# Cached pages with half of their keys already turned, and the samples' partial sums kept in DRAM

## The chip, the cores and the metric

The kernel runs on one core of one Trainium2 chip. The metric is the device time of one execution in microseconds. Three runs of the kernel before took 866.78, 866.91 and 869.01 us, median 866.91.

The engines named below: TensorE (PE in the profile; PEld is its weight load), VectorE (DVE), ScalarE (ACT), GpSimd (POOL) and SyncE (SP). SP computes nothing here: it issues most of the DMAs. GpSimd issues the others, and computes as well.

## The reference

One inference step of a decoder of two layers, for a prompt (512 tokens) and for eight samples of four tokens each, with the same weights. The change touches only the samples' part of the second layer: attention over a paged cache of 4,096 latent rows for each sample (32 pages of 128 rows, chosen by a page table) and over the four new rows. A row has 256 latent elements (`ckv`), which serve as keys and as values, and 64 rotary elements (`krope`), which serve as keys alone.

```python
ckv_past = cache_ckv[page_table].reshape(db, past, KV_RANK)        # 8 x 4096 x 256
krope_past = cache_krope[page_table].reshape(db, past, QK_ROPE)    # 8 x 4096 x 64
...
def mla_attend(q_lat, q_rope, ckv, krope, qpos, kpos):
    s = (jnp.einsum('bthc,bsc->bhts', q_lat, ckv)
         + jnp.einsum('bthr,bsr->bhts', q_rope, krope)) * MLA_SCALE
    mask = kpos[None, :] <= qpos[:, None]
    s = jnp.where(mask[None, None], s, -1e30)
    p = jax.nn.softmax(s, axis=-1)
    return jnp.einsum('bhts,bsc->bthc', p, ckv)
```

For one sample there are 32 queries (8 heads x 4 tokens). All is float32.

## The kernel before

**The whole.** Activations are kept transposed, features on the 128 partitions. Most products of the prompt are done as three float32r matmuls of a high and a low part (`mm3`, L92). Layer A and the start of layer B run first, in an order that the framework's scheduler sets by simulated times. From L915 on, the orders of TensorE and of SP are fixed by the program as it is written out (`pe_order`, `sp_order`); VectorE, ScalarE and GpSimd are still scheduled.

**The woven stage.** From L915 several threads (Python generators) are written out in turns by `weave` (L930): a thread yields the TensorE time that its step is reckoned to take and the time after which its next step may come; the thread that is furthest behind its share is taken next. The threads are `round_scores` and `round_values` (the samples' paged attention), `gates_late` (four gate projections), then `head_inputs` and `heads` (the prompt's eight heads), then `out_all` (the output projection). So the steps of the rounds stand between those of the other threads on TensorE, in a fixed order.

**A round.** There are 16 rounds: eight samples, two rounds each, 16 pages a round. A round is loaded in two halves of eight pages (`load_half`, L971). A half has one tile `nat`, 128 partitions x 8 pages x 320 columns (256 latent, 64 rotary); `nats` has four buffers, two rounds' worth. SP reads the eight page numbers from the list in SBUF into registers (L974), with a check of each against its bounds, and issues one DMA a page (L978). A page row is 1,280 bytes. The halves of round n + 2 are issued where `round_values` of round n has read the same buffers for the last time.

- `turn_keys` (L994): the latent rows have to be turned for the score matmul, whose contraction is over the latent elements. Four 128x128 transposes on TensorE (`transpose`, L133) into a PSUM bank `tr`, then a copy to an SBUF tile `kt` by ScalarE or VectorE (`kt_evac`, L983; two to one). A half needs four such groups: two parts of the latent dimension (k) by two groups of four pages (jp). `kt` has six buffers.
- scores (L1021, L1030): 16 matmuls a half into one bank `ac`: eight with the turned keys `kt` and the queries `QT`, 256 columns each, and eight with the rotary columns of `nat` (which are stored turned) and `Qr`.
- softmax of the round (L1039 to L1041): row maximum on VectorE, exponential with its sum on ScalarE into `rt`.
- values (L1051 to L1064): four transposes of the weights, a copy, and 16 matmuls with `nat` itself. The trace counts these f32 score and value matmuls twice each.
- after a sample's first round, ScalarE copies the sum to `ostore[:, b, :]`; after its second, VectorE rescales it and adds the second (L1083, L1084). `ostore` is one SBUF tile, 128 x 8 x 256.

**The end.** `combine` (L1436) merges the four page groups, the two rounds and the four new rows of all samples with `ostore` (L1495); `sample_out` (L1544) and `out_rows` (L1342) project. Weight slabs come by SP (`slab`, L1308); each is split into a high part by ScalarE and a low part by GpSimd (L88, L89). `mix_b` (L1294) splits the gated rows of the heads. Pools are stacks in SBUF: a pool that is opened after another has closed takes its memory, and waits for what used it.

**The host's side.** `_layouts` (L1610) rearranges the inputs before the launch; `cache_P` is the cache of pages with `ckv` and the turned `krope` side by side.

Of the kernel before, what the change touches and what calls it, by code (L numbers as in the profile page):

```python
# [7 lines left out]
F32 = mybir.dt.float32  # L8
# [20 lines left out]
PGW = 320  # L29
ULEN = PAD + SEQ + NB * (PAD + NT)  # L30
# [7 lines left out]
def trunk_kernel(ctx: ExitStack, tc: tile.TileContext, A, O):  # L38
# [751 lines left out]
    pg = Pool("pg", "right", g=(N, 9))  # L790
# [9 lines left out]
    nc.sync.dma_start(pages, A["page_list"])  # L800

# [166 lines left out]
    loaded, scored = {}, {}  # L968
    n_pool = A["cache_P"].shape[0]

    def load_half(n, ih):  # L971
        t = nats("nat").rearrange("p (s x) -> p s x", s=8)
        c = (2 * n + ih) * 8
        loads, own = nc.values_load_multi_w_load_instructions(  # L974
            pages[:, c : c + 8], [mybir.EngineType.SP], min_val=0, max_val=n_pool - 1
        )
        for g in range(8):
            nc.sync.dma_start(t[:, g, :], A["cache_P"][bass.ds(own[g], 1)].rearrange("n p x -> p (n x)"))  # L978
        loaded[n, ih] = t, now[0] + 9.0
# [10 lines left out]
    def round_scores():  # L990
        for n, (b, r) in enumerate(rounds):
            nat, kt = [None, None], {}

            def turn_keys(ih, k, jp):  # L994
                ps = ps_("tr")
                for g in range(4):
                    transpose(ps[:, g * P : (g + 1) * P], nat[ih][:, 4 * jp + g, k * P : (k + 1) * P])
                x = pro("kt")
                kt_evac(x, ps)
                kt[ih, jp, k] = x  # L1000
                return 0.44, 0.8

            ss = None
            for ih in range(2):
                if nat[ih] is None:
                    yield lambda: (n, ih) in loaded and loaded[n, ih][1] <= now[0]
                    nat[ih] = loaded[n, ih][0]
                for k in range(2):
                    for jp in range(2):
                        if (ih, jp, k) not in kt:  # L1010
                            yield turn_keys(ih, k, jp)
                if ih == 0 and (n, 1) in loaded and loaded[n, 1][1] <= now[0]:
                    nat[1] = loaded[n, 1][0]
                    yield turn_keys(1, 0, 0)
                else:
                    yield 0.0, 0.8
                ss = ss or ps_("ac")
                o = ss[:, ih * 256 : (ih + 1) * 256]
                for k in range(2):
                    for j in range(4):  # L1020
                        nc.tensor.matmul(  # L1021
                            o[j * NS : (j + 1) * NS, :],
                            lhsT=QT[:, k, b, :],
                            rhs=kt[ih, j // 2, k][:, j % 2 * 256 : (j % 2 + 1) * 256],
                            start=k == 0,
                            stop=False,
                        )
                for f in range(2):
                    for j in range(4):
                        nc.tensor.matmul(  # L1030
                            o[j * NS : (j + 1) * NS, :].rearrange("p (i f r) -> p f i r", i=2, f=2)[:, f],
                            lhsT=Qr[:, b, f, :],
                            rhs=nat[ih][:, 2 * j : 2 * j + 2, 256:],
                            start=False,
                            stop=f == 1,
                        )
                yield 1.3, 0.0
# [6 lines left out]
    def round_values():  # L1044
        first_part = None
        for n, (b, r) in enumerate(rounds):
# [9 lines left out]
            for i in range(4):  # L1056
                for j in range(4):
# [3 lines left out]
                        rhs=nat[i // 2][:, 2 * j + i % 2, :256],  # L1061
# [7 lines left out]
            if r == 0:  # L1069
                nc.scalar.copy(ostore[:, b, :], po[:, :256])  # L1070
                first_part = nx, sm
            else:
# [10 lines left out]
                nc.vector.tensor_scalar_mul(ostore[:, b, :], ostore[:, b, :], w[:, 2:3])  # L1083
                nc.vector.scalar_tensor_tensor(  # L1084
                    out=ostore[:, b, :], in0=po[:, :256], scalar=w[:, 3:4], in1=ostore[:, b, :], op0=ALU.mult, op1=ALU.add
                )
            yield 0.86, 0.0
# [29 lines left out]
    rs = Thread(round_scores(), 0.0, 1.0, 98.0)  # L1117
# [314 lines left out]
    cb = Pool("cb", "right", c=(96, 3), ws=(D, 5))  # L1432
# [3 lines left out]
    def combine(cb, v):  # L1436
# [7 lines left out]
        ms = pro("kt")  # L1444
# [19 lines left out]
        selw = pro("kt")  # L1464
# [6 lines left out]
        tz = pro("kt")  # L1471
# [11 lines left out]
        tt = pro("kt")  # L1483
# [3 lines left out]
        for bq in range(2):  # L1487
            for r in range(2):
                for b4 in range(4):
                    b = bq * 4 + b4  # L1490
                    if r == 0:
                        lhsT, rhs = selw[:, b * NS : (b + 1) * NS], ostore[:, b, :]
# [9 lines left out]
        on = pro("kt")  # L1502
# [5 lines left out]
        oT = pro("kt")  # L1508
# [22 lines left out]
        ov = pro("kt")  # L1531
# [78 lines left out]
def _layouts(a):  # L1610
# [29 lines left out]
                    a["cache_krope"].reshape(-1, 2, 64, 64).transpose(0, 1, 3, 2).reshape(-1, P, 64),  # L1640
                ],
# [75 lines left out]
```

## Time and profile before

| | |
|---|---|
| median of three runs | 866.91 us (866.78 to 869.01) |
| the profiled execution's own time | 867.66 us |
| its span, first to last instruction | 865.8 us |
| mean granted TensorE clock | 0.990 |
| bytes moved | 139.46 MB, of which pages 256 x 160 KB |
| the stage with the page rounds, from the first page load | 485.0 to 796.7 us |

How to read it: the page's first part gives the time each engine was busy. A row of its fifth part is a group of equal instructions: line, engine, operation, out<-in by the program's names, sizes and count; behind the bar the busy time, the mean in ns of one, and the idle time of the engine just before them with what ended it. Matmuls are pipelined, so what one costs in a row of others is the distance of their starts in the timeline and not its duration. The stage table gives each engine's busy time between two times; the waits list who waited for whom. In a timeline row the first number is the start and the second the time to the end of the merged piece, both in us. SPq and POOL rows with DMA are issues; the transfer follows on 16 DMA engines.

### The profile page before, as it was taken

To read this page: it belongs to the slowest core of one execution; us is meant where nothing else is said; L and a number is where in the kernel's file an instruction comes from. 1 tells how busy PE (TensorE), PEld (TensorE's weight loads), DVE (VectorE), ACT (ScalarE), POOL (GpSimd) and SP (SyncE) were. 2 spreads that over 40 slices of the span, in tenths; PEclk is the share of its full clock that TensorE was granted. 3 is DMA by queue.
4 is the path that set the end of the run, shared out by engine and by line. 5 is a ranking of instruction groups with operands and counts; after the bars stand their busy time and mean duration, and the time that the engine had idled before them with its cause. 6 is when DMAs were issued, how large, how long until landed. Compare 5 with 4: busy or idle time off the path is not lost.

```text
span 865.8 us, 18559 instructions
## 1 busy us (share of the span) xinstructions
PE 823.7 (95%) x7162; PEld 711.3 (82%) x7162; DVE 514.9 (59%) x961; ACT 349.9 (40%) x693; POOL 257.9 (30%) x206
## 2 busy tenths in 40 slices
PE   6999999989999999989999999989999999999996
PEld 6989989988999989769998986767778777777764
DVE  7766665987843444966766445575665657631603
ACT  7453433322433243444343235454544545442212
POOL 0044222633343323305323227150331400034421
PEclk9999999999999999999999999999999999999999
DMA  8355167311332326447228665645646564674742
GB/s 308 93 191 208 49 210 247 113 56 40 110 92 92 102 100 207 141 147 265 90 85 306 196 200 184 194 149 164 190 142 183 147 178 129 208 244 139 269 171 103
DMA packets 80858, 139.46 MB, mean 161 GB/s; under 512 B 9057, under 2 KB 49762, under 8 KB 80514
## 3 DMA queue, kind: packets, MB, share of 16 engines
q1 hardware_dynamic: 76258, 123.53, 44.8%
q0 software_dynamic: 4512, 14.75, 4.9%
q8 instruction: 56, 0.92, 0.4%
q14 instruction: 32, 0.26, 0.1%
HBM read 129.53 MB, written 8.72 MB: 160 GB/s over the span
## 4 chain that ended last, share of the span: by engine, by line
PE 51%; issue 7%; DVE 6%; DMA 3%; ACT 3%; SPq 1%; POOL 1%; POOLq 0%; ACTq 0%; DVEq 0%
PE pa L93 8%; PE pa L95 8%; PE pa L94 8%; PE tr L134 6%; PE oa L93 2%; PE ac L1021 2%; PE oa L94 2%; PE oa L95 2%; PE ac L1058 2%; PE ac L1030 1%; DVE t L744 1%; DMA wr<-in_w_mem_v 1%; SPq L978 1%; DMA ws<-in_w_out_b 1%; DMA wr<-in_w_out_b 1%
## 5 line engine op out<-in xcount | busy, mean ns | idle before, releaser
L93 PE MATMUL pa<-h,wh 128*128 128x272 f32 x832 | 241.6, 293 | 4.8 <-DVE g L612 4.5
L95 PE MATMUL pa<-h,wl 128*128 128x272 f32 x832 | 238.5, 291 | 1.9 <-POOL wl L89 1.9
L89 POOL TENSOR_TENSOR wl<-wr,wh 128x1024 fp32r<-128x1024 f32 (+1 forms) x67 | 156.5, 2337 | 249.6 <-ACT wh L88 233.0
L94 PE MATMUL pa<-h,wh 128*128 128x272 f32 x640 | 185.6, 291 | 0.0
L93 PEld LDWEIGHTS pa<-h,wh 128*128 128x128 f32 x832 | 158.2, 191 | 9.3 <-issue 5.2
L95 PEld LDWEIGHTS pa<-h,wl 128*128 128x128 f32 x832 | 157.0, 190 | 4.3 <-POOL wl L89 2.6
L88 ACT CAST wh<-wr 128x1024 fp32r<-128x1024 f32 (+1 forms) x87 | 87.7, 1009 | 166.0 <-PE pa L94 56.0
L94 PEld LDWEIGHTS pa<-h,wh 128*128 128x128 f32 x640 | 122.3, 191 | 1.0
L134 PE MATMUL tr<-c,nat 128*128 128x128 f32 x512 | 79.2, 280 | 5.3 <-DVE kt L988 3.9
L134 PEld LDWEIGHTS tr<-c,nat 128*128 128x128 f32 x512 | 59.1, 141 | 20.5 <-issue 7.3
L986 ACT COPY kt<-tr 128x512 f32<-128x512 f32 x86 | 50.4, 590 | 58.5 <-PE tr L134 58.0
L260 DVE SCALAR_TENSOR_TENSOR g<-t,g 128x272 f32<-128x272 f32 x48 | 50.0, 1048 | 14.4 <-ACT t L259 14.2
L94 PE MATMUL pa<-g,wh 128*128 128x272 f32 x192 | 54.5, 288 | 0.1
L259 ACT ACTIVATE t<-g 128x272 f32<-128x272 f32 x48 | 20.3, 429 | 73.0 <-DVE g L246 71.7
L988 DVE COPY kt<-tr 128x512 f32<-128x512 f32 x42 | 28.8, 686 | 23.2 <-PE tr L134 22.9
L93 PE MATMUL oa<-wh,c 128*128 128x512 f32 x96 | 39.8, 414 | 0.0
L94 PE MATMUL oa<-wl,c 128*128 128x512 f32 x96 | 38.0, 395 | 1.1 <-POOL wl L89 1.1
L246 DVE SCALAR_TENSOR_TENSOR g<-pa,r 128x272 f32<-128x272 f32 x42 | 18.1, 437 | 31.3 <-PE pa L95 31.3
L94 PEld LDWEIGHTS pa<-g,wh 128*128 128x128 f32 x192 | 36.1, 188 | 0.3 <-DVE g L89 0.3
L1021 PE MATMUL ac<-kt,c 128*32 128x256 f32 x512 | 35.6, 392 | 0.1
L89 DVE TENSOR_TENSOR wl<-wr,wh 128x1024 fp32r<-128x1024 f32 x20 | 24.5, 1224 | 12.8 <-ACT wh L88 12.7
L89 DVE TENSOR_TENSOR q<-q,q 128x512 fp32r<-128x512 f32 x16 | 25.2, 1574 | 11.2 <-ACT q L88 11.1
(367 smaller groups left out, 1706.1 us busy)
## 6 DMA issues: line engine op xcount, KB each, us to landing
nat<-in_cache_P SPq DMA_DIRECT2D x256, 160.0 KB, 3.0
wr<-in_w_in_a SPq DMA_DIRECT2D x24, 512.0 KB, 3.8
wr<-in_w_in_b SPq DMA_DIRECT2D x19, 512.0 KB, 3.7
cs<-in_mem_kT SPq DMA_DIRECT2D x16, 512.0 KB, 5.3
wr<-in_w_out_a SPq DMA_DIRECT2D x16, 384.0 KB, 3.0
wr<-in_w_out_b SPq DMA_DIRECT2D x12, 512.0 KB, 4.0
ws<-in_w_out_b SPq DMA_DIRECT2D x12, 512.0 KB, 5.6
wr<-in_w_mem_k SPq DMA_DIRECT2D x8, 512.0 KB, 3.9
```

Of the source, the lines that this page charges most:

```text
L88: nc.scalar.copy(h, src)
L89: (eng or nc.vector).tensor_tensor(out=l, in0=src, in1=fr(h), op=ALU.subtract)
L93: nc.tensor.matmul(out, lhsT=wh, rhs=xh, start=start, stop=False)
L94: nc.tensor.matmul(out, lhsT=wh, rhs=xl, start=False, stop=False)
L95: nc.tensor.matmul(out, lhsT=wl, rhs=xh, start=False, stop=stop)
L134: nc.tensor.transpose(out, in_, ident[:k, :k])
L246: nc.vector.scalar_tensor_tensor(out=out[:, o : o + HALF], in0=ps[:, :HALF], scalar=scale, in1=bc[:, o : o + HALF], op0=ALU.mult, op1=ALU. ...
L259: nc.scalar.activation(th[:, :HALF], z[:, o : o + HALF], AF.Tanh)
L260: nc.vector.scalar_tensor_tensor(out=z[:, o : o + HALF], in0=th[:, :HALF], scalar=1.0, in1=z[:, o : o + HALF], op0=ALU.add, op1=ALU.mult,)
L986: nc.scalar.copy(out, src)
L988: nc.vector.tensor_copy(out, src)
L1021: nc.tensor.matmul(o[j * NS : (j + 1) * NS, :], lhsT=QT[:, k, b, :], rhs=kt[ih, j // 2, k][:, j % 2 * 256 : (j % 2 + 1) * 256], start=k == ...
```

## The change

**Pages.** The host now lays the latent rows of a page a second time into `cache_P`, turned: a row of the cache has 576 columns, 320 as before and 256 of turned keys. Of the eight pages of a half, the first four are loaded with all 576 columns (2,304 bytes a row) into a tile `a`, the last four with 320 into a tile `b`. Scores of the first four read the turned keys from `a`, without transposes and copies; the last four are turned as before. So a half needs two groups of transposes where it had four. `kt` has three buffers.

**Partial sums.** `ostore` is a DRAM tensor. A sample's sum is kept in a small tile `os` (two buffers); after the second round GpSimd writes it to DRAM, for the first seven samples. At the end SP reads the seven back with one DMA into a tile `o`; the eighth is used where it is.

**Page list.** The list is clamped once on VectorE when it comes in, and the checks of each page number on SP are gone.

**Small moves.** `pg` has eight buffers instead of nine; the tiles of `mix_b` come from other pools; the tiles of `combine` come from a pool `cb` that is opened after the page tiles are closed; the planner's reckoning of a load and the rounds' share of its time are other numbers.

The diff, cut to its core:

```diff
@@ sample page list
 nc.sync.dma_start(pages, A["page_list"])
+n_pool = A["cache_P"].shape[0]
+nc.vector.tensor_scalar(out=pages, in0=pages, scalar1=0, scalar2=n_pool - 1, op0=ALU.max, op1=ALU.min)
@@ pools of the rounds
-pro = Pool("pro", "right", kt=(512, 6), rt=(512, 3), os=(2048, 1))
-nats = Pool("nats", "right", nat=(8 * PGW, 4))
+pro = Pool("pro", "right", kt=(512, 3), rt=(512, 3), os=(256, 2))
+nats = Pool("nats", "right", a=(4 * PGK, 4), b=(4 * PGW, 4))
-ostore = pro("os").rearrange("p (b c) -> p b c", b=NB)
+ostore = dram.tile([NB - 1, P, 256], F32, name="ostore")
@@ load_half
-t = nats("nat").rearrange("p (s x) -> p s x", s=8)
+half = [nats(tag).rearrange("p (s x) -> p s x", s=4) for tag in "ab"]
...
+    skip_runtime_bounds_check_because="the list is clamped on the chip when it comes in",
...
 for g in range(8):
-    nc.sync.dma_start(t[:, g, :], A["cache_P"][bass.ds(own[g], 1)].rearrange("n p x -> p (n x)"))
-loaded[n, ih] = t, now[0] + 9.0
+    t = half[g // 4][:, g % 4, :]
+    nc.sync.dma_start(t, A["cache_P"][bass.ds(own[g], 1), :, : t.shape[-1]].rearrange("n p x -> p (n x)"))
+issued[0] = max(issued[0], now[0]) + 6.4
+loaded[n, ih] = half, issued[0] + 5.0
@@ round_scores
 for k in range(2):
-    for jp in range(2):
-        if (ih, jp, k) not in kt:
-            yield turn_keys(ih, k, jp)
+    if (ih, k) not in kt:
+        yield turn_keys(ih, k)
...
-rhs=kt[ih, j // 2, k][:, j % 2 * 256 : (j % 2 + 1) * 256],
+rhs=(nat[ih][0][:, :, PGW + k * P : PGW + (k + 1) * P] if j < 2 else kt[ih, k])[
+    :, j % 2 * 2 : j % 2 * 2 + 2, :
+],
@@ round_values, after a sample's second round
+if b < NB - 1:
+    nc.gpsimd.dma_start(ostore[b], part)
+else:
+    parts[b] = part
@@ the planner
-rs = Thread(round_scores(), 0.0, 1.0, 98.0)
+rs = Thread(round_scores(), 0.0, 1.0, 70.0)
@@ mix_b
-    mixed[k] = split(pc("c", F32R), pt("t", F32R, SEQ), t)
+    mixed[k] = split(pc("c", F32R), pat("p", F32R), t)
-    mixed[k] = split(pc("c", F32R), pg("g", F32R, SEQ), gt[k][:, :SEQ])
+    mixed[k] = split(pc("c", F32R), (pg("g", F32R) if k else pt("t", F32R))[:, :SEQ], gt[k][:, :SEQ])
@@ sample_out
+o = cb("o").rearrange("p (b c) -> p b c", b=NB - 1)
+nc.sync.dma_start(o, ostore.rearrange("b p c -> p b c"))
+parts.update({b: o[:, b, :] for b in range(NB - 1)})
@@ _layouts, third part of cache_P
+a["cache_ckv"].reshape(-1, P, 2, P).transpose(0, 3, 2, 1).reshape(-1, P, 256),
```

What stands where, at three places. On TensorE, before, the first half's scores of the third round (turned keys `kt`, rotary columns of `nat_6386`), then the values of the second round, then the next transposes of a page tile:

```order
L1021 MATMUL ac_6760<-kt_6663,c_4069 32x256 x2
L1021 MATMUL ac_6760<-kt_6685,c_4069 32x256 x2
L1021 MATMUL ac_6760<-kt_6692,c_4069 32x256 x2
L1021 MATMUL ac_6760<-kt_6699,c_4069 32x256 x2
L1030 MATMUL ac_6760<-nat_6386,c_4070 32x2x64 x8
L1058 MATMUL ac_6777<-nat_5785,rt_6721 32x256 x8
L1058 MATMUL ac_6777<-nat_5867,rt_6721 32x256 x8
L134 MATMUL tr_6967<-c_79,nat_6476 128x128 x4
```

The same scores after the change (`a_6132` and `b_6133` are the half's two tiles):

```order
L1028 MATMUL ac_6444<-a_6132,c_4069 32x256 x2
L1028 MATMUL ac_6444<-kt_6301,c_4069 32x256 x2
L1028 MATMUL ac_6444<-a_6132,c_4069 32x256 x2
L1028 MATMUL ac_6444<-kt_6389,c_4069 32x256 x2
L1039 MATMUL ac_6444<-a_6132,c_4070 32x2x64 x2
L1039 MATMUL ac_6444<-b_6133,c_4070 32x2x64 x2
L1039 MATMUL ac_6444<-a_6132,c_4070 32x2x64 x2
L1039 MATMUL ac_6444<-b_6133,c_4070 32x2x64 x2
L135 MATMUL tr_6461<-c_79,b_6168 128x128 x4
```

Four of the eight score matmuls read the page tile itself, and there are two `kt` tiles where there were four; the second round's values stand earlier, ahead of these scores.

On SP, before, from the last page of the first half to the first of the second (`c_4072` is the page list; ISA rows are register and check instructions):

```order
L978 DMA nat_5621<-in_cache_P 128x320
L974 TENSOR_LOAD c_4072
L974 ISA x16
L978 ISA
L978 DMA nat_5703<-in_cache_P 128x320
```

And after:

```order
L985 DMA b_5623<-in_cache_P 128x320
L976 TENSOR_LOAD c_4072
L985 ISA
L985 DMA a_5649<-in_cache_P 128x576
L985 ISA
```

The 16 check instructions ahead of a half's first DMA are gone, 512 in all; the DMAs keep their places and their count.

On GpSimd, before, ahead of the first output slab's low part (`wl`), with the turned queries of the last heads (`qr`) and two loads of gates kept in DRAM:

```order
L1210 TENSOR_TENSOR qr_9901<-t_9893,qr_9901 64x512
L1210 TENSOR_TENSOR qr_9904<-t_9893,qr_9904 64x512
L1297 DMA tab_11983<-gmd 128x512
L1297 DMA tab_11989<-gmd 128x512
L89 TENSOR_TENSOR wl_11670<-wr_11667,wh_11669 128x1024
L89 TENSOR_TENSOR wl_11684<-wr_11681,wh_11683 128x1024
```

And after:

```order
L1224 TENSOR_TENSOR qr_8584<-t_8576,qr_8584 64x512
L1224 TENSOR_TENSOR qr_8587<-t_8576,qr_8587 64x512
L1098 DMA ostore<-os_8706 128x256
L1098 DMA ostore<-os_9196 128x256
L90 TENSOR_TENSOR wl_9519<-wr_9516,wh_9518 128x1024
L90 TENSOR_TENSOR wl_9533<-wr_9530,wh_9532 128x1024
```

The stores of the sixth and seventh sample's sums now stand there, and the two loads of gates behind the first slabs.

More of the change, by code (lines that the diff above doesn't have):

```diff
@@ L960, in ps_ @@
         return (rb if tag in rb.tags else hb)(tag)
-    pro = Pool("pro", "right", kt=(512, 6), rt=(512, 3), os=(2048, 1))
-    nats = Pool("nats", "right", nat=(8 * PGW, 4))
+    pro = Pool("pro", "right", kt=(512, 3), rt=(512, 3), os=(256, 2))
+    nats = Pool("nats", "right", a=(4 * PGK, 4), b=(4 * PGW, 4))
     stats_m = cst([P, NB])
     stats_s = cst([P, NB])
-    ostore = pro("os").rearrange("p (b c) -> p b c", b=NB)
+    ostore = dram.tile([NB - 1, P, 256], F32, name="ostore")
     rounds = [(b, r) for b in range(NB) for r in range(2)]
-    loaded, scored = {}, {}
-    n_pool = A["cache_P"].shape[0]
+    loaded, scored, parts, issued = {}, {}, {}, [0.0]
     def load_half(n, ih):
-        t = nats("nat").rearrange("p (s x) -> p s x", s=8)
+        half = [nats(tag).rearrange("p (s x) -> p s x", s=4) for tag in "ab"]
         c = (2 * n + ih) * 8
         loads, own = nc.values_load_multi_w_load_instructions(
-            pages[:, c : c + 8], [mybir.EngineType.SP], min_val=0, max_val=n_pool - 1
+            pages[:, c : c + 8],
+            [mybir.EngineType.SP],
+            min_val=0,
+            max_val=n_pool - 1,
+            skip_runtime_bounds_check_because="the list is clamped on the chip when it comes in",
         )
         for g in range(8):
-            nc.sync.dma_start(t[:, g, :], A["cache_P"][bass.ds(own[g], 1)].rearrange("n p x -> p (n x)"))
-        loaded[n, ih] = t, now[0] + 9.0
+            t = half[g // 4][:, g % 4, :]
+            nc.sync.dma_start(t, A["cache_P"][bass.ds(own[g], 1), :, : t.shape[-1]].rearrange("n p x -> p (n x)"))
+        issued[0] = max(issued[0], now[0]) + 6.4
+        loaded[n, ih] = half, issued[0] + 5.0
     even = [0]
@@ L992, in round_scores, with turn_keys @@
             nat, kt = [None, None], {}
-            def turn_keys(ih, k, jp):
+            def turn_keys(ih, k):
                 ps = ps_("tr")
                 for g in range(4):
-                    transpose(ps[:, g * P : (g + 1) * P], nat[ih][:, 4 * jp + g, k * P : (k + 1) * P])
+                    transpose(ps[:, g * P : (g + 1) * P], nat[ih][1][:, g, k * P : (k + 1) * P])
                 x = pro("kt")
                 kt_evac(x, ps)
-                kt[ih, jp, k] = x
+                kt[ih, k] = x.rearrange("p (s c) -> p s c", s=4)
                 return 0.44, 0.8
@@ L1032, in round_scores @@
                             lhsT=Qr[:, b, f, :],
-                            rhs=nat[ih][:, 2 * j : 2 * j + 2, 256:],
+                            rhs=nat[ih][j // 2][:, j % 2 * 2 : j % 2 * 2 + 2, 256:PGW],
                             start=False,
@@ L1060, in round_values @@
                         lhsT=pT[:, i * P + j * NS : i * P + (j + 1) * NS],
-                        rhs=nat[i // 2][:, 2 * j + i % 2, :256],
+                        rhs=nat[i // 2][j // 2][:, j % 2 * 2 + i % 2, :256],
                         start=i == 0,
@@ L1069, in round_values @@
             if r == 0:
-                nc.scalar.copy(ostore[:, b, :], po[:, :256])
+                part = pro("os")
+                nc.scalar.copy(part, po[:, :256])
                 first_part = nx, sm
@@ L1082, in round_values @@
                 nc.vector.scalar_tensor_tensor(out=sc, in0=sm, scalar=w[:, 3:4], in1=sc, op0=ALU.mult, op1=ALU.add)
-                nc.vector.tensor_scalar_mul(ostore[:, b, :], ostore[:, b, :], w[:, 2:3])
+                nc.vector.tensor_scalar_mul(part, part, w[:, 2:3])
                 nc.vector.scalar_tensor_tensor(
-                    out=ostore[:, b, :], in0=po[:, :256], scalar=w[:, 3:4], in1=ostore[:, b, :], op0=ALU.mult, op1=ALU.add
+                    out=part, in0=po[:, :256], scalar=w[:, 3:4], in1=part, op0=ALU.mult, op1=ALU.add
                 )
+                if b < NB - 1:
+                    nc.gpsimd.dma_start(ostore[b], part)
+                else:
+                    parts[b] = part
             yield 0.86, 0.0
```

23 lines of the change are left out of this document (12 added, 11 removed).

## The prediction

> **What bounds the kernel now.** The page first, its top and the costliest groups; then the time by stage, for the change touches one stage.
>
> ```profile
> span 865.8 us, 18559 instructions
> PE 823.7 (95%) x7162; PEld 711.3 (82%) x7162; DVE 514.9 (59%) x961; ACT 349.9 (40%) x693; POOL 257.9 (30%) x206
> ...
> L134 PE MATMUL tr<-c,nat 128*128 128x128 f32 x512 | 79.2, 280 | 5.3 <-DVE kt L988 3.9
> ...
> L986 ACT COPY kt<-tr 128x512 f32<-128x512 f32 x86 | 50.4, 590 | 58.5 <-PE tr L134 58.0
> ```
>
> TensorE is busy 95% of the span; no other engine passes 59%. The 512 transposes of cached pages (L134 into tr from nat) are what the change halves. Their 280 ns each is pipelined time, so it can't be multiplied; starts have to be compared, below. The transposes belong to one stage:
>
> ```profile
> L134 PE MATMUL tr<-c,nat x512: 270/273/421, 495.1 to 781.8; 128*128 128x128 f32 x171
> L1058 PE MATMUL ac<-nat,rt x512: 379/379/403, 521.9 to 796.7; 128*32 128x256 f32 x171
> L978 SPq DMA_DIRECT2D nat<-in_cache_P x256: 332/333/1678, 485.0 to 761.6; - x128
> ```
>
> From the tile view of the page tiles: loads from 485.0, first transpose at 495.1, last value matmul at 796.7: 301.6 us for 16 rounds, 18.9 us a round. The columns of the stage table are PE, PEld, DVE, ACT and POOL busy, clock, DMA share, GB/s.
>
> ```profile
> 540.00:580.00 40.00, 37.91 (x416) 28.63 (x409) 24.24 (x58) 19.98 (x46) 11.96 (x12) 1.00 0.54 160
> 580.00:620.00 40.00, 38.18 (x383) 29.64 (x383) 24.85 (x56) 19.98 (x45) 8.35 (x10) 1.00 0.64 188
> ```
>
> TensorE idles 2 us in 40, VectorE is at 61%, ScalarE at 50%, the DMA engines at 54 and 64%. From the waits of TensorE in 440 to 800 us (in total, times, longest), the three on pages and turned keys:
>
> ```profile
> PE tr L134 <- DVE kt L988: 3.9, 4, 1.7
> PE tr L134 <- ACT kt L986: 2.2, 6, 0.7
> PE tr L134 <- DMA nat<-in_cache_P: 0.3, 2, 0.2
> ```
>
> So the stage is TensorE's own work, in an order written by hand, and a page is late by 0.3 us in all. Work taken off TensorE here shortens the span, unless a load then comes late.
>
> **The transposes.** 64 groups of four go, with 64 copies (43 on ScalarE at 590 ns, 21 on VectorE, by the counts in the two orders). What a group costs shows in the starts:
>
> ```profile
> 613.32 1.07 PE L1021 MATMUL ac<-kt,c 128*32 128x256 f32 x16
> 614.20 0.62 PE L1030 MATMUL ac<-nat,c 128*32 128x128 f32 x16
> 614.75 0.66 PE L134 MATMUL tr<-c,nat 128*128 128x128 f32 x4
> 615.25 0.60 PE L134 MATMUL hs<-c,e 128*128 128x128 f32 x4
> ...
> 616.38 0.60 PE L134 MATMUL tr<-c,nat 128*128 128x128 f32 x4
> 616.74 0.48 PE L93 MATMUL pa<-c,wuh 128*128 128x512 f32 x1
> 617.05 0.39 PE L94 MATMUL pa<-c,wuh 128*128 128x512 f32 x1
> 617.28 0.40 PE L95 MATMUL pa<-c,wul 128*128 128x512 f32 x1
> ```
>
> Behind a score block a group takes 0.50 us (614.75 to 615.25), between projections 0.36 (616.38 to 616.74), and the matmul behind it 0.31 instead of 0.23. That bounds 64 groups by 23 and 32 us; between them I take 0.42 a group, **27 us**. The score matmuls that now read half of the keys straight from the page tile keep their count and 256 columns, in two pieces of 128. L1021 reads 256 columns in one piece, 16 in 0.88 us; L1030 reads 128 in pieces of 64, 16 in 0.55, so 0.11 more than half of L1021. If two pieces cost that on all 16 blocks that now read pages, it is 2 x 0.11 x 16 = 3.5 us; I take 0, since the 0.55 ends at a change of operation and these pieces are twice as long. Of the 6.1 us of waiting for turned keys, half the copies take half away: 0 to 6, I take **3 us**. kt falls from six buffers to three; a round needs four, but the fourth is filled after the first half's scores have read the first two, so nothing new waits.
>
> **The pages.** A half round is 8 pages: 1.31 MB before, 4 x 295 KB and 4 x 164 KB = 1.84 MB now, in the same four buffers, and one queue. How fast rows move:
>
> ```profile
> DMA packets 1684, 1.95 MB, mean 177 GB/s; under 512 B 179, under 2 KB 1682, under 8 KB 1682
> q1 hardware_dynamic: 1682, 1.92, 60.6%
> ...
> DMA packets 1613, 3.58 MB, mean 358 GB/s; under 512 B 209, under 2 KB 209, under 8 KB 1613
> q1 hardware_dynamic: 1613, 3.58, 100.0%
> ```
>
> The first pair is the DMA view of 542 to 553 us, page rows of 1,280 B: 60.6% of 16 engines x 11 us over 1,682 packets is 63 ns each, for 1,141 B on average. The second is 2 to 12 us, rows of 2 and 4 KB: 99 ns for 2,220 B. A line through both (33 ns per KB) gives 68 ns for 1,280 B and 102 for 2,304 B, estimates. With 8 rows an engine a wide page takes 0.82 us, a narrow one 0.54, a half 5.4 us; two halves 10.9 of a round of about 17. Issue:
>
> ```profile
> 760.06 0.33 SPq L978
> 760.58 0.33 SPq L978
> ...
> 557.02 11.55 SPq L978 DMA_DIRECT2D nat<-in_cache_P  x16
> ...
> L974 SPq FUSED_REGOPS  x256: 147/147/186, 476.8 to 757.5; - x128
> ...
> nat<-in_cache_P SPq DMA_DIRECT2D x256, 160.0 KB, 3.0
> ```
>
> The chain has a page issued each 0.52 us, so eight in 4.2; with the checks between the halves 16 took 11.55. Before, counted from the first issue, a first half has landed at 7 x 0.52 + 3.0 = 6.6 us, a second at 11.55 - 0.33 + 3.0 = 14.2. After it the checks are gone (8 x 0.147 = 1.2 us a half, off SP alone) and the data set the pace: 5.4 + 2.5 = 7.9 (2.5 is the 3.0 less a page's own 0.54), and 7.9 + 5.4 = 13.3. So the **first half lands 1.3 us later, the second 0.9 earlier**. What was there to spare, from one round before:
>
> ```profile
> 540.64 1.91 PE L1058 MATMUL ac<-nat,rt 128*32 128x256 f32 x32
> 541.74 18.19 SPq L978 DMA_DIRECT2D nat<-in_cache_P  x22
> 549.67 1.03 PE L134 MATMUL tr<-c,nat 128*128 128x128 f32 x8
> ```
>
> The first 16 of L1058 free a buffer, SP issues at 541.74, and TensorE reads the first half at 549.67: 7.9 us, 1.3 more than the landing. In the new order two of the page groups that stood in this stretch are gone, some 1.0 us, and its first transpose reads the narrow pages, loaded last: 6.9 against 7.9, **1.0 us short**. Bounds over 14 loaded rounds: 0, and 14 us if all are like this one. I take **4 us**: a late round moves the following loads and reads alike, and the work between differs from round to round. The Trainium skill's "DMA: Bandwidth & Descriptors", section "Anatomy of one DMA — SWDGE (gpsimd) path", fits a transfer as 2.0 us and its bytes at 436 GB/s; by that rate a half is 4.2 us, no page is late and the sum below is 4 us less. The rows above show 2.22 KB in 99 ns on 16 engines, 359 GB/s, and no such rate.
>
> **The end and the rest.** In both orders the first output slab stands behind the last page on SP:
>
> ```profile
> 762.04 5.67 DMA wr<-in_w_out_b
> 768.92 2.38 POOL wl L89
> ...
> PE oa L94 <- POOL wl L89: 1.1, 1, 1.1
> ...
> 814.20 0.64 PE L1495 MATMUL tr<-os,kt 128*32 128x256 f32 x8
> ...
> 800.00:815.00 15.00, 15.00 (x80) 11.02 (x82) 9.37 (x16) 5.62 (x12) 8.96 (x8) 1.00 0.97 339
> ```
>
> Slab, cast and difference take 9.3 us from 762.04 (to 768.92 + 2.38), and TensorE already waits 1.1 us for them. The slab now queues behind a transfer of 1.3 us more, on a shorter round: 1 to 3 us more wait. The read of the stored sums (917 KB) falls where the DMA engines are 97% busy at 339 GB/s: 2.7 us of transfer, wanted only by the final sum, which began 17.5 us after the last value matmul (796.7). Together 0 to 5, I take **2**. The seven stores from GpSimd stand on an engine 30% busy, in front of splits loaded two ahead: 0, and if a store waits for a late VectorE sum, up to 1 us each on the split behind it. Fewer fillers between a head's scores and its softmax: 0 to 4, I take **1**. The clamp:
>
> ```profile
> 10.11 0.31 SPq L800 DMA_DIRECT2D c<-in_page_list  x1
> 21.30 1.27 DVE L301 SCALAR_TENSOR_TENSOR ml<-x,c,mh 128x256 fp32r<-128x256 f32 x3
> 23.88 0.16 DVE L187 COPY s<-tr 128x4 f32<-128x4 f32 x1 [1.30 <-PE tr L184]
> ```
>
> It stands just ahead of L301 on VectorE, 11 us after the list was asked for, and VectorE then idles 1.30 us: 0.
>
> **The sum.** 27 + 3 gained, 4 + 2 + 1 given back: 23 us off the profiled execution's own 867.7 (span 865.8 and 1.9 around it) is 844.7; the median of the runs is 0.8 lower, so **844**.
>
> **Rivals.** *Page transfers set the pace (slower).* The first half of each of 14 loaded rounds is waited for; once those waits sum to 27 us, 1.9 a round, the transposes are paid back. With the 6.9 us above that point is a half in 6.9 + 1.9 - 2.5 = 6.3 us, 291 GB/s. For it: the 580 to 620 stage moved 188 GB/s at 0.64, 294 when busy, with narrow rows. If halves took 7.0 us in every round, 14 x 2.6 = 36 us of waits give 867.7 - 30 + 36 + 3 = 877; range 867 to 885. Against it: wide rows cost less per byte in the rows above, and it needs every round as tight as the one shown. The Trainium skill's "TensorE: Matmul & The Clock Gate", section "HAM oscillation — how this bites in real kernels", would add to it: idle gaps beyond about 3.4 us drop the array's clock to half. Here the clock reads 1.00 in both stages, with waits for keys up to 1.7 us; no wait priced here reaches 3.4. By that rule each longer gap would cost about 3.4 us again; 0.01 of this rival's chance stands for it.
>
> *A smaller gain.* Waits for pages of 0.9 to 1.7 us a round, 12 to 24 us where the forecast has 4: 852 to 864.
>
> *The transposes were filler.* If they only covered softmax and copy latencies, TensorE idles instead and the time stays at 867. Against it: it idles just 5%, and a head's softmax has projections and value matmuls to cover it as well.
>
> *More than forecast.* Groups at 0.50 and no page late: under 836.
>
> **How the numbers follow.** Forecast (836 to 852) 0.70; smaller gain 0.15; filler 0.04; page-bound and slower 0.07; more than forecast 0.04. A measurement of this kernel tells about 0.3% (2.6 us) from no change: faster 0.89, same 0.04, slower 0.07. The range leaves out the slower rival, filler, the best case and the upper third of the smaller gain: 836 to 860.
>
> **What would show it.** 256 transposes of pages; the stage from first transpose to last value matmul near 277 us; TensorE still busy over 90% in it; its waits for pages 2 to 8 us in all, most for a first half; DMA share near 0.75 to 0.8. Wrong if the waits for pages exceed 15 us, if the wide pages land far apart, or if TensorE idles on VectorE or ScalarE instead.

## The result, and the profile after

The changed kernel takes **838.92 us** (median of 4 runs, 836.92 to 840.85) against 867.48 (866.78 to 869.01) for the kernel before on the same chip: ratio 0.9668, 95% interval 0.964 to 0.9697. That is 28.6 us or 3.3% faster. The profiled execution took 836.92 us, with a span of 835.2.

The top of the page after, with the two groups that the change halves (busy us, mean ns, idle before them):

```profile
span 835.2 us, 17542 instructions
PE 792.8 (95%) x6906; PEld 680.8 (82%) x6906; DVE 506.1 (61%) x941; ACT 326.9 (39%) x650; POOL 262.4 (31%) x213
...
L135 PE MATMUL tr<-c,b 128*128 128x128 f32 x256 | 40.0, 277 | 3.0 <-DVE kt L996 1.7
...
L994 ACT COPY kt<-tr 128x512 f32<-128x512 f32 x43 | 25.3, 589 | 27.0 <-PE tr L135 26.0
```

TensorE's busy time fell by 30.9 us and the span by 30.6; its idle time (span less busy) is 42.4 us and was 42.1. So the work that was taken off was on the path, and nothing took its place. Not all of the 30.9 is the change's: the mean granted clock of this execution is 0.994 and was 0.990, and 0.004 of 824 us is some 3 us. That belongs to these two executions: the four runs of the changed kernel have 0.986 to 0.994. The tile view of the narrow page tile `b` after gives the stage:

```profile
L135 PE MATMUL tr<-c,b x256: 270/272/330, 494.5 to 738.6; 128*128 128x128 f32 x128
...
L1067 PE MATMUL ac<-b,rt x256: 379/379/403, 515.9 to 761.9; 128*32 128x256 f32 x128
...
  DMA b<-in_cache_P: 2.2, 6
```

From the first transpose to the last value matmul it is now 267.4 us, and was 301.6: 34.2 less. What follows the stage grew from 69.1 to 73.3 us, since 12 output matmuls that stood among the rounds (0.235 us each, 2.8 us) now stand behind them, and the stored sums are waited for (1.1 us, below). The last row says that TensorE and its weight loads idled 2.2 us, 6 times, until a narrow page came; the same row for the wide tile `a` reads 1.6 us, 5 times, and for `nat` before 1.1, 4 times.

TensorE's waits from 485 to 800 us after (in total, times, longest), without the rows under 0.8 but one:

```profile
PE tr L135 <- DVE kt L996: 1.7, 1, 1.7
PE tr L135 <- ACT rt L1050: 1.6, 2, 1.1
PE pa L94 <- DVE q L1206: 1.3, 3, 0.6
PE tr L1509 <- DMA o<-ostore: 1.1, 1, 1.1
PE pa L94 <- DVE c L1091: 1.1, 1, 1.1
PE hs L1257 <- POOL qr L1224: 0.9, 1, 0.9
PE tr L135 <- ACT kt L994: 0.8, 1, 0.8
...
PE tr L135 <- DMA b<-in_cache_P: 0.4, 1, 0.4
```

Waits for turned keys are 2.5 us where they were 6.1; three rows are new, for `rt`, `c` and `qr`, 3.6 us together; and the read-back of the stored sums is waited for at the end, 1.1 us. The stretches that were shown of before (PE, PEld, DVE, ACT, POOL busy, clock, DMA share, GB/s):

```profile
540.00:580.00 40.00, 37.83 (x402) 27.17 (x396) 25.90 (x55) 19.21 (x45) 14.82 (x16) 1.00 0.72 242
580.00:620.00 40.00, 39.02 (x419) 29.28 (x412) 22.66 (x53) 16.66 (x41) 11.68 (x12) 1.00 0.83 272
```

The DMA engines move 242 and 272 GB/s where they moved 160 and 188, and TensorE is no less busy.

### The profile page after: what moved, and what is told of

It is laid out like the page before. It is cut to its first block, busy times and chain, and to the rows that moved or that the text cites. A ratio compares the mean times of both kernels' runs of the same rounds, so it can differ in the third digit from the quotient of the medians.

```text
span 835.2 us, 17542 instructions
## 1 busy us (share of the span) xinstructions
PE 792.8 (95%) x6906; PEld 680.8 (82%) x6906; DVE 506.1 (61%) x941; ACT 326.9 (39%) x650; POOL 262.4 (31%) x213
## 4 chain that ended last, share of the span: by engine, by line
PE 73%; DVE 10%; DMA 8%; issue 3%; ACT 3%; POOL 2%; SPq 1%; POOLq 0%; DVEq 0%; ACTq 0%
PE pa L94 14%; PE pa L96 14%; PE pa L95 14%; PE tr L135 5%; PE ac L1028 3%; PE ac L1067 3%; DVE v L583 2%; DMA o<-ostore 2%; PE oa L94 2%; PE oa L95 2%; DMA b<-in_cache_P 2%; PE oa L96 2%; PE ac L1039 1%; PE ac L389 1%; SPq L985 1%
## 5 line engine op out<-in xcount | busy, mean ns | idle before, releaser
L135 PE MATMUL tr<-c,b 128*128 128x128 f32 x256 | 40.0, 277 | 3.0 <-DVE kt L996 1.7
L135 PEld LDWEIGHTS tr<-c,b 128*128 128x128 f32 x256 | 29.7, 140 | 9.7 <-issue 3.0
L994 ACT COPY kt<-tr 128x512 f32<-128x512 f32 x43 | 25.3, 589 | 27.0 <-PE tr L135 26.0
L1028 PE MATMUL ac<-a,c 128*32 128x256 f32 x256 | 34.7, 392 | 0.0
L90 DVE TENSOR_TENSOR q<-q,q 128x512 fp32r<-128x512 f32 x16 | 27.2, 1700 | 10.0 <-ACT q L89 9.9
```

The lines of the kernel that those rows point to most:

```text
L90: (eng or nc.vector).tensor_tensor(out=l, in0=src, in1=fr(h), op=ALU.subtract)
L135: nc.tensor.transpose(out, in_, ident[:k, :k])
L994: nc.scalar.copy(out, src)
L1028: nc.tensor.matmul(o[j * NS : (j + 1) * NS, :], lhsT=QT[:, k, b, :], rhs=(nat[ih][0][:, :, PGW + k * P : PGW + (k + 1) * P] if j < 2 else ...
```

## The experiments

Two questions are behind them. Is the gain the transposes alone? And why are the wide pages not late, when the round shown in the prediction left them 1.0 us short? **Theory**: the gain is TensorE time saved, and the pages are hidden by the distance between a free buffer and its next read. **Rivals**: other parts of the change (the clamp, the new order) made the gain; or the pages do cost, and something else pays for them. Ratios are to the kernel before, with 95% intervals; where two kernels are compared by their medians, both have the kernel before beside them within 1 us (866.48 to 867.48).

### The transposes put back

```
+ def spare_turn(ih, k): four transposes of the first four pages into tr, no copy
  for k in range(2):
+     yield spare_turn(ih, k)
- rs = Thread(round_scores(), 0.0, 1.0, 70.0)
+ rs = Thread(round_scores(), 0.0, 1.0, 98.0)
```

> The changed kernel, with the 64 transpose groups of the first four pages put back on TensorE into a PSUM bank that nothing reads: no copies, the same wide pages. Theory (the gain is TensorE's own time for the 256 transposes, 0.445 us a group): 28 us come back, 864 to 869 us. Rival (part of the gain is the 64 copies and the waits for them): only 15 to 22 us come back, 853 to 861 us.

Measured: 863.76 us (860.23 to 865.32), ratio 0.9967 (0.9946 to 0.9988). 256 transposes that nobody reads cost **24.8 us**, 0.39 a group: just under the theory's range, above the rival's. From the first transpose of a narrow page to the last value matmul the stage took 289.3 us. The page shows what it is made of:

```profile
PE 820.9 (96%) x7162; PEld 710.9 (83%) x7162; DVE 497.1 (58%) x941; ACT 328.0 (38%) x650; POOL 261.8 (30%) x213
```

TensorE is busy 28.1 us more than in the changed kernel (some 4 of them by the clock, 0.989 for 0.994), but idle only 37.9 us of a span of 858.8, 4.5 less: the spare transposes also fill waits. So most of the gain is TensorE time; what is not in it is 3.8 us of the 28.6, or 2.7 against the 866.48 us of the kernel before beside this run.

### No wide pages at all

```
- nats = Pool("nats", "right", a=(4 * PGK, 4), b=(4 * PGW, 4))
+ nats = Pool("nats", "right", a=(4 * PGW, 4), b=(4 * PGW, 4))
- rhs=(nat[ih][0][:, :, PGW + k * P : PGW + (k + 1) * P] if j < 2 else kt[ih, k])[
+ rhs=(nat[ih][0][:, :, k * P : (k + 1) * P] if j < 2 else kt[ih, k])[
```

This leaves out the turning of the first four pages: their scores read unturned columns.

> The changed kernel with all eight pages of a half narrow (320 columns); the scores of the first four read the unturned latent columns, so the turning of those pages' keys is left out. Theory (the wide rows are hidden, because the new order reads a half later): 837 to 840 us, no measurable change against the changed kernel. Rival (the wide rows cost the 4 us that the prediction gave them): 833 to 836 us.

Measured: 842.69 us (841.14 to 843.74), ratio 0.9726 (0.9687 to 0.9766). It has 16.8 MB less to load (128 pages x 131 KB), no wait for a narrow page, and is not faster: its time is above both ranges. What it lost instead is shown at the run on the issue order, below: the scheduler put rows of ScalarE, VectorE and GpSimd in another order. So it bounds the cost of wide pages only roughly, at nothing that can be told.

### The clamp alone, the new reckoning alone, and both

All three are the kernel before, with narrow pages and all its transposes.

```
x3, y6:
+ nc.vector.tensor_scalar(out=pages, in0=pages, scalar1=0, scalar2=n_pool - 1, op0=ALU.max, op1=ALU.min)
+     skip_runtime_bounds_check_because=...
y5, y6:
- loaded[n, ih] = t, now[0] + 9.0
+ issued[0] = max(issued[0], now[0]) + 6.4
+ loaded[n, ih] = t, issued[0] + 5.0
```

> The kernel before, with the page list clamped once and the checks on SP taken out; nothing else. Theory (SP waits for buffers anyway, so its checks cost nothing): 866 to 869 us. Rival (second halves are issued 1.2 us earlier and TensorE gets its pages sooner): 860 to 864 us.

> The kernel before with one edit: its planner reckons a half ready at issue plus 6.4 plus 5.0, as in the changed kernel, in place of now plus 9.0. All pages stay narrow and all keys are turned on TensorE. Theory (the order only spaces the reads; TensorE waited 1.1 us for pages before, so there is nothing to gain): 864 to 868 us. Rival (the new order is itself a part of the 28 us): 858 to 863 us.

> The kernel before with the clamp in place of the run-time checks and with the new reckoning: everything of the change that is not the wide pages or the stored sums. All keys are turned on TensorE. Alone the first was worth 3.3 us (863.18 against 866.48) and the second 3.6 us (863.63 against 867.18). Theory (they work in different places, the issue of the pages and the order of TensorE's work, and add): 859 to 861.5 us. Rival (both only take away the same 1.1 us of waits for pages and what follows from them): 862.5 to 865 us.

Measured: 863.18 us for the clamp (ratio 0.9962, 0.9943 to 0.9982), 863.63 for the reckoning (0.9958, 0.9943 to 0.9973), and 865.63 for both (0.9981, 0.9967 to 0.9994). The clamp came out in its rival's range, against the theory; the reckoning just above its rival's. Each alone is worth some 3 us, and together they are worth 1.3: neither "add" nor "the same wait" is right. For the reckoning the page shows a part of it:

```profile
PE 818.5 (95%) x7162; PEld 708.5 (82%) x7162; DVE 508.3 (59%) x961; ACT 350.6 (41%) x693; POOL 257.4 (30%) x206
```

The same 7162 matmuls keep TensorE busy 5.2 us less than before (823.7). About half of that is the clock, 0.993 in this execution and 0.990 before: 0.003 of 820 us is 2.5. Most of the rest is in the page transposes, the distances of whose starts sum to 55.0 us here and 57.0 before. Why is not shown: changes between float32r products and f32 matmuls are not fewer, 242 in the last 3,462 matmuls here and 228 before. Where both together lose 2.0 us against the reckoning alone, one place stands out. First the timeline of TensorE, then that of ScalarE, in the run with both:

```profile
748.11 1.07 PE L134 MATMUL tr<-c,nat 128*128 128x128 f32 x4 [3.88 <-ACT kt L989]
```

```profile
746.53 1.04 ACT L88 CAST wh<-wr 128x1024 fp32r<-128x1024 f32 x1 [4.27 <-DMA wr<-in_w_out_b]
747.48 0.58 ACT L989 COPY kt<-tr 128x512 f32<-128x512 f32 x1
```

The cast of an output slab stands ahead of a copy of turned keys on ScalarE, it starts after a wait of 4.27 us for the slab, the copy starts behind it, and TensorE waits 3.88 for the copy. TensorE's order is the same as with the reckoning alone; on ScalarE only the places of two copies and two casts differ: there both copies stood ahead of the first cast, here one is behind the first and one behind the second. The reckoning alone pays there too, once, for a softmax cast that stands behind three slab casts:

```profile
754.80 0.50 PE L99 MATMUL po<-p,vx 128*128 128x512 f32 x1 [2.97 <-ACT p L88]
```

So the place costs some 1.4 us more waiting (3.88 and 0.47 against 2.97), and the clock from 735 to 770 us is 0.90 where it is 0.95, some 1.7 us. Together that more than covers the 2.0 us. The 3 us of the clamp alone can't be given to the checks for the same reason: its rows on ScalarE are in another order too.

### The order without the new reckoning

```
- issued[0] = max(issued[0], now[0]) + 6.4
- loaded[n, ih] = half, issued[0] + 5.0
+ loaded[n, ih] = half, now[0] + 9.0
```

> The changed kernel, with the planner told that every half load is there 9.0 after its issue, as in the kernel before, in place of loads that follow one another at 6.4 and land 5.0 later. Theory (the reckoning made the order read a half later, 7.0 to 13.3 us after its buffer is free, and so hid the wide pages): first reads come earlier, TensorE's waits for pages grow from 0.4 to 5 to 15 us, 843 to 853 us. Rival (the order would have hidden them either way): 837 to 841 us.

Measured: **895.74 us** (892.88 to 898.68), ratio 1.0346 (1.03 to 1.0391): slower than before, on one reckoning of the planner. The theory had the sign, and at its upper end 14 of the 56.8 us. From the tile view of `b`:

```profile
L1066 PE MATMUL ac<-b,rt x256: 379/379/637, 514.3 to 791.9; 128*32 128x256 f32 x128
...
  DMA b<-in_cache_P: 43.6, 79
...
DMA to landing us min/median/max: 3.5/5.0/8.7
```

A page lands 5.0 us after its DMA starts, and in the changed kernel 4.9. The pages are as fast; TensorE reads them sooner, and it and its weight loads idle 43.6 us in 79 places, 23.8 of them TensorE's matmuls themselves. Sooner is above all the second half of a round: from the value matmul that frees its buffer to its first transpose it has a median of 12.0 us here and 16.4 in the changed kernel, a first half 8.8 and 10.0. And 17.7 of the 23.8 us stand ahead of second halves. With the waits the clock falls. TensorE's wait, and the stretches around it (the clock is the third number from the right):

```profile
606.25 1.62 PE L135 MATMUL tr<-c,b 128*128 128x128 f32 x4 [4.33 <-DMA b<-in_cache_P]
```

```profile
604.00:606.00 2.00, 0.00 (x0) 0.00 (x0) 0.01 (x1) 0.00 (x0) 0.00 (x0) 0.81 0.75 271
606.00:608.00 2.00, 1.75 (x6) 1.16 (x7) 0.10 (x1) 0.00 (x0) 0.00 (x0) 0.50 0.07 24
608.00:610.00 2.00, 2.00 (x15) 1.35 (x17) 1.38 (x3) 0.48 (x1) 0.00 (x0) 0.50 0.00 0
610.00:612.00 2.00, 2.00 (x28) 0.96 (x20) 0.46 (x1) 0.00 (x0) 0.00 (x0) 0.50 0.00 0
```

The mean clock is 0.968 and was 0.994 in the changed kernel. Waits of 40 us more and 0.026 of 891 us, 23 us, cover the 56.8 between the two kernels, with some overlap. So the order that the new reckoning sets is what hides the wide pages, second halves first of all.

### The checks put back

```
-     skip_runtime_bounds_check_because=...
```

> The changed kernel with the run-time checks of the page indices put back on SP; the clamp of the list stays. The clamp without checks was worth 3.3 us in the kernel before (863.18 against 866.48). Theory (the 256 checks delay the issue of the pages, and that is worth as much here): 841 to 844 us, with TensorE waiting for pages some us more. Rival (in the new order a half is read some 2 us longer after its buffer came free, so a later issue is hidden): 838 to 840 us, no difference that can be told.

Measured: **845.63 us** (844.94 to 848.86), ratio 0.9757 (0.9733 to 0.9781), apart from the changed kernel's 0.964 to 0.9697: 6.7 us slower, above both ranges. TensorE's order is the same, row for row; on ScalarE, VectorE and GpSimd two casts, a copy and a difference have other places. The narrow tile's row, and two halves of one round as SP issues them, first here, then in the changed kernel:

```profile
  DMA b<-in_cache_P: 9.4, 21
```

```profile
597.71 1.88 SPq L984 DMA_DIRECT2D b<-in_cache_P  x4
602.45 1.89 SPq L984 DMA_DIRECT2D a<-in_cache_P  x4
```

```profile
596.93 1.88 SPq L985 DMA_DIRECT2D b<-in_cache_P  x4
599.64 1.89 SPq L985 DMA_DIRECT2D a<-in_cache_P  x4
```

Between the last page of a half and the first of the next SP needs 2.86 us with the checks (597.71 + 1.88 to 602.45) and 0.83 without. Waits for narrow pages grow from 2.2 to 9.4 us, 7.2, about the loss of the medians. (The profiled execution itself took 848.86 us, 11.9 more; its clock, 0.988 for 0.994, is 5 of them.) So the later issue can account for the 6.7 us; what the other places of those few rows add is not shown. SP's own slack shows in its waits for a page buffer, with the checks, then without:

```profile
SPq L984 <- PE ac L1066: 28.0, 10, 5.6
```

```profile
SPq L985 <- PE ac L1067: 74.4, 14, 11.0
```

### More to load

```
+ nc.sync.dma_start(spare[2 * n + ih], A["cache_P"][:4])     # ahead of each half
```

> The changed kernel with one more transfer ahead of each half's pages on SP's queue: four wide pages (1.18 MB) from the cache to a buffer in DRAM that nobody reads. It asks how much later the pages may land. At the 242 to 272 GB/s of the middle stretches a half's 1.84 MB and this are 3.0 MB or 11 to 12.5 us for a half whose work on TensorE takes some 8.4 us. Theory (transfers become the bound of the stage): 925 to 970 us, TensorE waiting for pages some 90 us or more. Rival (the transfers have room, since the 16 DMA engines are not full in these stretches, and the pages land 3 to 4 us later): 845 to 860 us, waits for pages of 10 to 25 us.

Measured: 881.92 us (879.21 to 885.25), ratio 1.0188 (1.0164 to 1.0211): between the two. Two stretches of the stage and a row of the tile view of `b`:

```profile
495.00:540.00 45.00, 39.76 (x386) 30.93 (x385) 20.40 (x34) 13.80 (x30) 18.14 (x19) 0.96 1.02 378
660.00:700.00 40.00, 37.26 (x374) 28.90 (x377) 24.70 (x56) 15.92 (x38) 10.12 (x10) 0.97 1.00 365
```

```profile
  DMA b<-in_cache_P: 26.8, 56
```

The DMA engines are full and move 365 to 378 GB/s; my expectation had taken 242 to 272, a demand, for the limit. At 365 GB/s the changed kernel's half of 1.84 MB takes 5.0 us of the 8.4 that TensorE has for it (267.4 over 32 halves); with 1.18 MB more it takes 8.3, and there, at the edge, 43.0 us are lost. Not all by the bytes: the clock, 0.977 for 0.994, is some 15 of them, and SP held its page loads 46.5 us in all until the added transfers had landed.

### The read-back first, and the narrow pages first

```
x7, x11:  the read of ostore ahead of the five slabs
x11:
- for g in range(8):
+ for g in (4, 5, 6, 7, 0, 1, 2, 3):
```

> The changed kernel with the read-back of the stored sums issued on SP ahead of the five slabs of the end, not behind them. Theory (the 1.1 us that TensorE waits for the read-back at the end go, nothing else is late): 837.0 to 838.5 us, the wait at line 1509 for the DMA gone. Rival (the slabs land that much later and are waited for in its place, or the stores that the read-back waits for hold SP): 838.5 to 841 us.

> The changed kernel with a half's four narrow pages issued ahead of its four wide ones, since a round turns the narrow ones before it scores any; and with the read-back of the sums ahead of the slabs (837.61 us alone). Theory (the 2.6 us that TensorE and its weight loads wait for the narrow pages go): 834.5 to 836.5 us. Rival (the wide pages, asked for last, are waited for in their place, or the waits were hidden): 837 to 840 us.

Measured: 837.61 us (836.4 to 839.1), ratio 0.9664, with the read-back first; the 1.1 us wait for it is gone, and the 1.3 us by which the median is lower can't be told from none. With the narrow pages first as well, 842.14 us (839.8 to 843.69), ratio 0.9719 (0.9697 to 0.9741), 4.5 slower and above both ranges, though no narrow page is waited for any more and the wide ones only 1.0 us. The loss is near 530 us. ScalarE there with the narrow pages first, and the wait of TensorE that follows:

```profile
535.05 0.59 ACT L994 COPY kt<-tr 128x512 f32<-128x512 f32 x1 [2.49 <-PE tr L135]
536.46 0.59 ACT L89 CAST vx<-pa 128x512 fp32r<-128x512 f32 x1 [0.83 <-PE pa L96]
536.94 1.25 ACT L1223 CAST qr<-t 64x512 fp32r<-64x512 f32 x2
```

```profile
538.95 0.44 PE L1257 MATMUL hs<-c,qr 128*128 128x128 f32 x1 [2.25 <-POOL qr L1224]
```

And ScalarE with only the read-back moved:

```profile
533.51 0.59 ACT L994 COPY kt<-tr 128x512 f32<-128x512 f32 x1 [2.30 <-PE tr L135]
533.99 1.26 ACT L1223 CAST qr<-t 64x512 fp32r<-64x512 f32 x2
535.27 0.58 ACT L89 CAST vx<-pa 128x512 fp32r<-128x512 f32 x1
```

TensorE's rows are the same in both kernels. On ScalarE the cast to `vx` has gone ahead of the two to `qr`; GpSimd's subtraction for `qr` (L1224) starts behind them, and TensorE waits 2.25 us where it waited 0.88. A few rows before, VectorE's order differs too, and a wait for `q` is 2.29 where it was 0.39. The kernel without wide pages has the same swap of `vx` and `qr` and the same two waits (in all 3.5 for `q`, 2.2 for `qr`), and a clock of 0.988 where the changed kernel has 0.994; so it can't show what the wide rows alone cost.

### One step further

```
- a=(4 * PGK, 4), b=(4 * PGW, 4)
+ a=(4 * PGK, 4), c=(2 * (PGW + P), 4), b=(2 * PGW, 4)
  pages 4 and 5 of a half: scores of k = 0 read turned keys from c; 6 of the 8 transposes of pages 4 to 7 are left
- kt=(512, 3) ... os=(256, 2); small s=(16, 24)
+ k0=(256, 2), k1=(512, 1) ... os=(256, 1); small s=(16, 20); the read of ostore first
- rs = Thread(round_scores(), 0.0, 1.0, 70.0)
+ rs = Thread(round_scores(), 0.0, 1.0, 63.0)
x12 only:
- for g in range(8):
+ for g in (6, 7, 4, 5, 0, 1, 2, 3):
```

> One step further than the changed kernel: of each half, pages 4 and 5 also come with the first 128 rows of their keys turned (a tile of 448 columns for the two), so that of a half's 16 turnings 6 are left in place of 8; the read-back goes first as in the run before. Turned keys of the first 128 rows have 2 buffers and those of the second 128 rows 1, and the small tiles 20 in place of 24, so that it fits. Theory (64 transposes fewer at 24.8 us for the 256 that the spare turnings put back, so 6.2 us; a half's data grows by 131 KB on 1,835, some 7%, hidden by the distance between free buffer and first read): 831 to 835 us. Rival (the single buffer of turned keys or the wider pages give it back): 838 to 846 us, with waits for kt's buffer or for pages of over 5 us.

> The kernel with ten of sixteen pages of a half in the turned form or half of it (847.02 us, TensorE and its weight loads waiting 11.7 us for the narrow pages), with the pages that are turned first issued first. Theory (its loss is these waits): 834 to 839 us, waits for pages under 4 us. Rival (its loss is the single buffer of turned keys and the smaller pools, and pages only where they are asked for last): 842 to 847 us.

Measured: 847.02 us (842.58 to 847.69), ratio 0.9765, in the old order of issue; **835.71** (834.87 to 837.62), ratio 0.9649 (0.9628 to 0.9669), with the pages that are turned first issued first. From the tile views, the narrow tile in the first, the wide tile in the second:

```profile
  DMA b<-in_cache_P: 11.7, 10
```

```profile
  DMA a<-in_cache_P: 2.7, 7
```

In the second no narrow page is waited for. TensorE's rows are the same in the two, VectorE's and GpSimd's too, and ScalarE's differ in one: 11.3 us for an order of issue (the clock, 0.985 and 0.989, is some 3 of them). Of the 6.2 us that 64 transposes fewer should give against 837.61, 1.9 are there. The second kernel has the lowest median of all here, 31.2 us under the kernel before beside it; its interval overlaps that of the changed kernel, so that it is faster than that one isn't shown.

## Why the prediction was right, and where it was off

The forecast was 844 us, 5.1 over the result; the sign, the stage and the mechanism were right. By its steps:

| step | put at | the runs |
|---|---|---|
| transposes | -27 | -24.8 by the spare transposes; -28.3 by the distances of their starts (57.0 us before, 28.7 after) |
| waits for turned keys | -3 | 6.1 to 2.5: -3.6 |
| wide pages | +4 | +2.7 (1.1 to 2.2 + 1.6), weight loads included; TensorE's matmuls alone 0.3 to 0.4 |
| the end | +2 | +1.1, the read-back; the slab wait did not grow (1.1 to 0.7) |
| fewer fillers | +1 | +3.6, the waits for `rt`, `c` and `qr` |
| GpSimd's stores | 0 | up to 0.6 of the 0.9 for `qr`: a store of 0.55 us at 531.21 stands just ahead of it on GpSimd |
| scores in two pieces | 0 | 0: the starts of the 256-column score matmuls sum to 28.6 us before and 28.3 after |
| checks off SP | 0 | 6.7 us faster than the new kernel with them, see below |
| TensorE's clock | not in the sum | some -3 between the two profiled executions (0.990 to 0.994) |

- **The transposes** were right within their bounds, and so was the view that they were read in: starts, not the 280 ns.
- **The waits** are where most of the 5.1 us lie. Keys, pages, end and fillers were put at -3, +4, +2 and +1, together +4; TensorE's idle time went from 42.1 to 42.4 us. Pages and end cost less than priced, keys gave a little more, and the missing fillers cost more: the errors partly cancel. All other matmuls gave nothing: without waits and at full clock the distances of their starts sum to 761 us in both kernels.
- **The checks** were mis-sized. The prediction wrote "the checks are gone (8 x 0.147 = 1.2 us a half, off SP alone) and the data set the pace". With the checks back the pages are issued 2.0 us a half later, not 1.2, and 7.2 us of waits for pages come of it. But the +4 for pages was worked out for a kernel without checks, so the 6.7 us do not go on top of the sum. That the kernel with them, 845.63 us, lies 1.6 off the forecast is chance as far as the runs show.
- **The pages** were mis-sized in their base. I took one round, 7.9 us from free buffer to first read, and carried it to the new order as 6.9. Before, this distance was 6.6 to 11.3 us in the 14 loaded rounds; after, the timeline has it at 7.0 to 13.3, with a median near 10, and only the round at 7.0 waits on TensorE's side. The order is written from the planner's reckoning of the loads, which the change also edits, and I had not asked what that edit does to the distance. The run with the old reckoning shows what it is worth: 56.8 us. It shows too what the prediction left out: its rival let only first halves be waited for, and there three quarters of TensorE's waits are for second halves.
- **The slower rival** was priced at 877 with a chance of 0.07. Pages can set the pace, and its price was too low: with the old reckoning 895.74, with two thirds more data 881.92, in part by a clock that falls with the waits. That it didn't come is due to the planner's new reckoning, not to the rates of rows. The rate that the prediction gave as the point, 291 GB/s, is one that the DMA engines pass when asked: 365 to 378.
- The prediction weighed a rule of the Trainium skill's "DMA: Bandwidth & Descriptors", section "Anatomy of one DMA — SWDGE (gpsimd) path", 436 GB/s for the bytes of a transfer (its fit is of transfers that GpSimd issues; these come from SP). The two stretches shown with full DMA engines moved 365 and 378 GB/s, at DMA shares of 1.00 and 1.02. The measured rate decides. The sum by that rule, 840, lies nearer to the result than 844, and that no page would be late came out nearly true, but for another reason.
- **What would show it**: 256 transposes, yes; the stage near 277 us, 267.4; TensorE over 90% busy, yes; waits for pages 2 to 8 us, 3.8 with the weight loads'; DMA share 0.75 to 0.8, 0.72 and 0.83.

What stays open: the 3.3 us of the clamp alone and the 3.6 of the reckoning alone in the kernel before are of the size by which a few rows in another order on ScalarE move this kernel, so neither is shown to be its cause's own. What the wide rows cost by themselves in the new order is open for the same reason.

## What to carry to other kernels

When a change makes loads longer, look first at what sets the distance between a free buffer and its next read: here one reckoning of a planner was worth twice the gain, and the order in which a half's pages were issued 11 us in one kernel, with 4.5 lost beside it in another. Work taken off the engine that issues loads is not free of effect because that engine waits; price it as an earlier issue of every load. Before a smaller busy time is put down to an order, compare the clocks of the two executions. And where other engines are scheduled by simulated times, compare their rows before giving 3 us to a cause: a few rows in another order came with 2 to 4.5 us three times here.

## What was not expected of the hardware

The prediction said of the clock that no wait priced there reaches the 3.4 us at which the Trainium skill's "TensorE: Matmul & The Clock Gate", section "HAM oscillation — how this bites in real kernels", has it drop. The run with the narrow pages first shows it after less: TensorE waits 1.07 and 2.29 us, with 2.8 us of work between them, and later 2.25 alone. The stretches behind each:

```profile
528.00:530.00 2.00, 1.00 (x2) 0.84 (x3) 1.91 (x4) 0.62 (x1) 1.98 (x4) 0.69 1.03 369
530.00:532.00 2.00, 2.00 (x7) 1.50 (x6) 1.69 (x1) 0.03 (x1) 1.13 (x1) 0.50 1.06 389
532.00:534.00 2.00, 2.00 (x32) 1.26 (x34) 1.29 (x2) 0.55 (x1) 0.00 (x0) 0.95 0.99 361
...
538.00:540.00 2.00, 1.05 (x5) 1.05 (x6) 0.32 (x2) 0.20 (x1) 1.93 (x2) 0.75 0.92 300
540.00:542.00 2.00, 2.00 (x18) 1.09 (x21) 1.22 (x5) 0.85 (x4) 0.25 (x1) 0.50 1.02 372
542.00:544.00 2.00, 2.00 (x33) 1.57 (x26) 0.52 (x2) 0.51 (x3) 0.00 (x0) 0.89 1.06 378
```

By the shares of the stretches the clock is at 0.50 for some 3.4 us each time (0.31, 0.50 and 0.05 of full speed are missing in three stretches of 2 us, 1.7 us in all), and that is 1.7 us of work again on top of a wait of 2.3. The prediction had reckoned 3.4 us for a drop. Here the measurement differs from the rule and decides: a wait of 2.3 us among others was enough. The wait of 4.33 us with the old reckoning was followed by some 6.8 us at 0.50.

The kernel before shows more. After a wait of 1.67 us that ends at 348.55 its clock is 0.90, 0.50 and 0.75 in the three stretches from 348 to 354 us. And near 756 us it falls while TensorE is busy throughout, behind 3.0 us (752.7 to 755.7) of matmuls of four columns:

```profile
754.00:756.00 2.00, 2.00 (x32) 1.82 (x30) 0.23 (x3) 0.21 (x2) 0.00 (x0) 0.94 0.91 270
756.00:758.00 2.00, 2.00 (x16) 1.44 (x16) 1.05 (x5) 0.71 (x2) 0.00 (x0) 0.50 0.41 136
758.00:760.00 2.00, 2.00 (x34) 1.11 (x27) 0.48 (x3) 0.00 (x0) 0.00 (x0) 0.70 0.43 120
```

The missing shares are again 1.7 us. With the reckoning alone, on the other hand, the clock stays at 1.00 after the wait of 2.97 us. So below 3 us the length of a wait does not decide by itself in these runs.
